# Latent attention in a two-layer encoder: rotary products, turns and key norms put into a fixed order, and two more empty products at the start

## The chip, the cores and the metric

The kernel runs on one core of a Trainium2 chip. The metric is the device time of one execution in microseconds (us). The engines are TensorE (PE, with its weight loads as PEld), VectorE (DVE), ScalarE (ACT), GpSimd (POOL) and SyncE (SP, which here only issues DMAs).

## What is computed

Two layers on a sequence of 256 positions with 1024 channels, float32. Each layer is half a SwiGLU FFN (width 2816), a mixer, and half a SwiGLU FFN, each with an RMSNorm ahead of it. The mixer of layer 0 is a convolution module; that of layer 1 is the latent attention that the change is about:

```python
def mla(h, positions, w_a, g_q, g_kv, w_uq, w_ukv, w_o):
    a = h @ w_a                                   # 512 + 256 + 64 columns
    c_q = rmsnorm(a[..., :Q_LORA], g_q)
    c_kv = rmsnorm(a[..., Q_LORA:Q_LORA + KV_LORA], g_kv)
    k_rope = a[..., Q_LORA + KV_LORA:]
    q = jnp.einsum("bsc,chd->bshd", c_q, w_uq)    # 8 heads of 128 + 64
    q_nope, q_rope = q[..., :QK_NOPE], q[..., QK_NOPE:]
    kv = jnp.einsum("bsc,chd->bshd", c_kv, w_ukv) # 8 heads of 128 + 128
    k_nope, v = kv[..., :QK_NOPE], kv[..., QK_NOPE:]
    ...
    q_rope = apply_rope(q_rope, cos[:, :, None, :], sin[:, :, None, :])
    k_rope = apply_rope(k_rope, cos, sin)
    ... # scores of both parts, block-causal softmax in chunks of 64, values
    return o.reshape(o.shape[0], seq, N_HEADS * V_HEAD) @ w_o
```

## The kernel before, in words

The 256 positions are two tiles of 128 rows, `tb` 0 and 1. Every float32 product is done as three products of split operands (`mm3`, L269, L272, L273): a weight block `raw` of 128x2048 comes by a DMA on SP's queue (1 MB), ACT writes its rounded part `hi` (L185) and DVE the rest `lo` (L186), each in two pieces of 1024 columns; the other operand is split in the same way. There are three buffers for `raw` and five for `hi` and `lo`. The weight blocks of the whole kernel are one list, in the order of their use. `weights(n, more)` takes the next n of them, and `load_ahead(k)` writes the DMAs and casts of all blocks up to k beyond those taken. For attention the list is: four blocks of `w_a`, then `wuq[2]` (rotary part of all heads), `wuq[0]` (plain part, heads 0 to 3), `wukv[0]` (keys), `wukv[1]` (values), `wuq[1]` (heads 4 to 7), and four blocks of `wo`.

The order of instructions on an engine is set by a planner: it simulates the program with costs of its own and takes, for each engine, the instruction that is ready and first in priority, which is the order in which the program is written. Functions marked `@urgent` get a higher priority. `order(a, b)` pins a behind b on the same engine; it adds no waiting on the chip. A weight cast is pinned behind the last six urgent instructions written before it on its engine (`behind`). On the chip each engine then works off its list in that order, and an instruction that waits holds up what stands behind it.

Around the change, attention goes like this. `low` makes the products with `w_a` into banks `a`: for each `tb` first the 512 query columns, then the 320 key columns. `normed` squares them on ACT (`squares`, L296), makes the factor on POOL (`power`, L304, L305, L307; `rr`, L1149), and scales on DVE (`cn`, L1151). The results are `cq[tb]` and `ck[tb]`. `key_rope` rotates the 64 shared key columns into `kd[tb]` on DVE. `split_rows` turns a normed tile: PE transposes it in pieces of 128x128 (`transposed`, L313, tile `tp`, "turns" below), ACT writes the high parts (L328) and DVE the low parts (L332), into `CQh` and `CQl` (one tile, `CQ`) for the queries and `CKh` and `CKl` for the keys. There are three banks for turns (B) and four for products (A).

Then come the rotary products `qr`, 12 for each `tb`, and `rope` on DVE (L1093, L1095, L1100), which writes `qrope`; the plain query products for four heads (`nope` into `QN`); the turns of `kd` and `qrope`; the key products (`nope` into `KN`); the values (`v`); and the scores. Before the change only the start of the rotary products was fixed by what they need; the turns, the norms and the second half of the rotary products were placed by the planner.

At its start the kernel runs `WARM` empty products (`keep_warm`, L261, 128x256, bf16, zeros) while the first weights come in.

Of the kernel before, what the change touches and what calls it, by code (L numbers as in the profile page):

```python
# [21 lines left out]
S = 256  # L22
NT = S // P
# [8 lines left out]
H = 8  # L32
NOPE = 128
ROPE = 64
VH = 128
QL = 512
KVL = 256
# [1 line left out]
EPS = 1e-6  # L39
RAW_BUFS = 3  # L40
W_BUFS = 5
WARM = 20
PIECES = 2

BEHIND = 6
# [17 lines left out]
GCOL = {}  # L63
# [19 lines left out]
def trunk(ctx: ExitStack, tc: tile.TileContext, x, xt, pos, invf, gains, gfin, wdw,  # L83
# [21 lines left out]
    def bank(tag, name):  # L105
        return ps.tile([P, 512], F32, tag=tag, name=uid(name), bufs=BANKS[tag])
# [28 lines left out]
    def order(ins, first):  # L135
        tc.add_manual_dep(ins.ins, first.name, mybir.DependencyInfo(
            mybir.DependencyClass.NoSync, mybir.DependencyReason.DATA), reason="order")
# [66 lines left out]
    def load_ahead(ahead=W_BUFS - 2):  # L204
        load_to(min(len(blocks), n_used[0] + ahead))
# [5 lines left out]
    def weights(n=1, more=True):  # L211
        out = []
        for _ in range(n):
            n_used[0] += 1
            if more:
                load_ahead()
            else:
                load_ahead(0)
            out.append(loaded[n_used[0] - 1])
        return out  # L220
# [46 lines left out]
    def mm3(o, ah, al, bh, bl, start, stop, after=()):  # L267

        mm = nc.tensor.matmul(o, ah, bl, start=start, stop=False)  # L269
        for a in after:  # L270
            order(mm, a.ins)
        nc.tensor.matmul(o, ah, bh, start=False, stop=False)  # L272
        return nc.tensor.matmul(o, al, bh, start=False, stop=stop)  # L273
# [8 lines left out]
    def tbs(tb):  # L282
        return slice(tb * P, (tb + 1) * P)
# [9 lines left out]
    def squares(ss, src, n, i, scale_in=1.0, after=()):  # L293
        nh = n // 2
        junk = tmp.tile([P, 512], F32, tag="s", name=uid("junk"))
        sq = nc.scalar.activation(junk[:, :nh], src[:, i * nh:(i + 1) * nh], AF.Square, scale=scale_in,  # L296
                                  accum_out=ss[:, i:i + 1])
        for a in after:
            order(sq, a.ins)
        return sq  # L300
# [9 lines left out]
    def transposed(src, q, n, after=(), turned=None):  # L310
        b = bank("B", "tp")
        for j in range(n):
            tp = nc.tensor.transpose(b[:, j * P:(j + 1) * P], src[:, (q + j) * P:(q + j + 1) * P], ident)  # L313
            if turned is not None:
                turned.append(tp)
            for a in after:
                order(tp, a.ins)
        return b

    @urgent  # L320
    def split_rows(src, q, n, gcol, dh, dl, tb, after=(), low_after=(), turned=None,
                   lows=None):

        b = transposed(src, q, n, after, turned)
        for j in range(n):
            k = q + j
            g = G[:, gcol + k:gcol + k + 1]
            high = nc.scalar.activation(dh[:, k, tbs(tb)], b[:, j * P:(j + 1) * P], AF.Copy, scale=g)  # L328
        for j in range(n):
            k = q + j  # L330
            g = G[:, gcol + k:gcol + k + 1]
            low = nc.vector.scalar_tensor_tensor(dl[:, k, tbs(tb)], b[:, j * P:(j + 1) * P], g,  # L332
                                                 dh[:, k, tbs(tb)].bitcast(F32), op0=ALU.mult, op1=ALU.subtract)
            if lows is not None:
                lows.append(low)
            for a in low_after:
                order(low, a.ins)
        return high
# [768 lines left out]
    def mla_in(act, X, make_next, cc, sn):  # L1107
        R = X.r
# [18 lines left out]
        def low(parts, w, tb, last):  # L1127
            u = bank("A", "a")
            for a in range(2):
                hi, lo = parts[a]  # L1130
                for j in range(4):
                    k = 4 * a + j
                    last_low[0] = mm3(u[:, :w], X.xh[:, k, tbs(tb)], X.xl[:, k, tbs(tb)], hi[:, j * w:(j + 1) * w],
                                      lo[:, j * w:(j + 1) * w], k == 0, k == KT - 1,
                                      (last,) if last is not None and k == 0 else ())
            return u

        @urgent
        def normed(u, n, tb, between=None):
            ss = small.tile([P, 2], F32, tag="ss", name=uid("ss"))  # L1140
            for i in range(2):
                sq = squares(ss, u[:, :n], n, i, R[tb])
            if between is not None:
                between()
                for high in X.highs[4:]:
                    order(high, sq.ins)
            r2 = power(ss, n, "r2")
            rr = small.tile([P, 1], F32, tag="rr", name=uid("rr"))
            nc.gpsimd.tensor_tensor(rr, r2, R[tb], op=ALU.mult)  # L1149
            cn = act.tile([P, n], F32, tag=f"cn{n}", name=uid("cn"), bufs=2)  # L1150
            scaled = nc.vector.tensor_scalar(cn, u[:, :n], rr, None, op0=ALU.mult)  # L1151
            if between is not None:
                order(scaled, X.ends[1].ins)
            return cn

        def key_rope(u, tb):
            kx = act.tile([P, 64], F32, tag="kx", name=uid("kx"), bufs=2)
            nc.vector.tensor_scalar(kx, u[:, KVL:KVL + ROPE], R[tb], None, op0=ALU.mult)
            kd = act.tile([P, 2, 64], F32, tag="kd", name=uid("kd"), bufs=2)
            for i in range(2):  # L1160
                rope(act, kd[:, i, :], kx.rearrange("p (n i f) -> p n i f", n=1, i=2), 1, cc, sn, tb)
            return kd.rearrange("p i f -> p (i f)")
# [4 lines left out]
        cq, ck, kd = [], [], []  # L1167
        last = None
        for tb in range(NT):
            for i, w in enumerate((QL, KVL + ROPE)):  # L1170
                u = low(parts[2 * i:2 * i + 2], w, tb, last)
                last = last_low[0]
                if tb == 0 and i == 1:
                    X.end(0)
                    load_ahead(1)
                if i == 0:
                    cq.append(normed(u, QL, tb))
                    if tb == 1:
                        load_ahead()
                else:  # L1180
                    if tb == 0:

                        ck.append(normed(u, KVL, tb, lambda: X.late(1)))
                    else:
                        ck.append(normed(u, KVL, tb))
                    kd.append(key_rope(u, tb))
                if tb == 1 and i == 1:
                    split_rows(cq[0], 0, 4, GCOL["q"], CQh, CQl, 0)


        QR = act.tile([P, 4, S], F32, tag="QR", name="QR")
# [1 line left out]
        QN = xp.tile([P, H, S], F32, tag="Xl", name="QN")  # L1193
        VV = act.tile([P, NT, H * VH], F32, tag="VV", name="VV")

        def nope(part, dst, nk, ch, cl, width, h0, heads):

            hi, lo = part
            for i in range(heads[0], heads[1], 2):
                b = bank("A", "nope")  # L1200
                for e in range(2):
                    for k in range(nk):
                        c = slice(k * width + (i + e) * P, k * width + (i + e + 1) * P)
                        mm3(b[:, e * S:(e + 1) * S], hi[:, c], lo[:, c], ch[:, k, :], cl[:, k, :],
                            k == 0, k == nk - 1)
                nc.scalar.copy(dst[:, h0 + i:h0 + i + 2, :], b.rearrange("p (e t) -> p e t", t=S))


        (hi, lo), = weights()
        qr = []  # L1210
        for tb in range(NT):
            u = bank("A", "qr")
            for k in range(4):
                mm3(u, CQh[:, k, tbs(tb)], CQl[:, k, tbs(tb)], hi[:, k * 512:(k + 1) * 512],
                    lo[:, k * 512:(k + 1) * 512], k == 0, k == 3)
            if tb == 0:
                lows = []
                split_rows(cq[1], 0, 4, GCOL["q"], CQh, CQl, 1, lows=lows)
                for t in range(NT):
                    split_rows(ck[t], 0, 2, GCOL["kv"], CKh, CKl, t, lows=lows)  # L1220
            q = act.tile([P, 512], F32, tag="cn512", name=uid("qrope"), bufs=2)
            rope(act, q, u.rearrange("p (n i f) -> p n i f", i=2, f=32), H, cc, sn, tb, lows)
            qr.append(q)
        part, = weights()
        nope(part, QN, 4, CQh, CQl, 512, 0, (0, 4))
        for t in range(NT):
            b = transposed(kd[t], 0, 1)
            for i in range(2):
                half = slice(64 * i, 64 * i + 64)
                nc.scalar.copy(KR[half, i, tbs(t)], b[half, :P])  # L1230
        for tb in range(NT):
            b = transposed(qr[tb], 0, 4)
            nc.scalar.copy(QR[:, :, tbs(tb)], b.rearrange("p (j t) -> p j t", t=P))
        kpart, = weights()
        nope(kpart, KN, 2, CKh, CKl, D, 0, (0, H))
# [208 lines left out]
```

## Time and profile before

| | |
|---|---|
| Runs | 929.58 us median of 3 (929.41, 929.58, 931.34) |
| Profiled execution | 931.24 us, span 929.4 us |
| PE busy | 915.6 us, 99% of the span |
| DVE, ACT, POOL busy | 589.8, 494.2, 123.6 us |
| Granted TensorE clock, mean | 0.994 |
| DMA | 194.73 MB, mean 210 GB/s |
| First rotary product | 662.31 us from the span's start |
| First key product | 682.40 us |

Times in the views are counted from the start of the span, which is 1.8 us shorter than the time of the same execution. In a timeline each row has start, duration, engine, line, operation, output<-inputs, shape and count; the bracket is the idle time of the engine before it and what ended that. Products of PE overlap, so the time that one costs is the distance from start to start. The granted clock is given as a share of full speed.

### The profile page before, as it was taken

To read this page: it belongs to the slowest core of one execution; us is meant where nothing else is said; L and a number is where in the kernel's file an instruction comes from. 1 tells how busy PE (TensorE), PEld (TensorE's weight loads), DVE (VectorE), ACT (ScalarE), POOL (GpSimd) and SP (SyncE) were. 2 spreads that over 40 slices of the span, in tenths; PEclk is the share of its full clock that TensorE was granted. 3 is DMA by queue.
4 is the path that set the end of the run, shared out by engine and by line. 5 is a ranking of instruction groups with operands and counts; after the bars stand their busy time and mean duration, and the time that the engine had idled before them with its cause. 6 is when DMAs were issued, how large, how long until landed. Compare 5 with 4: busy or idle time off the path is not lost.

```text
span 929.4 us, 12106 instructions
## 1 busy us (share of the span) xinstructions
PE 915.6 (99%) x4346; PEld 767.7 (83%) x4346; DVE 589.8 (63%) x931; ACT 494.2 (53%) x844; POOL 123.6 (13%) x255
## 2 busy tenths in 40 slices
PE   9999999999999999999999999999799999999997
PEld 7888888898978888888888888888698888888886
DVE  5895764489987666654576556545746686656633
ACT  7564544488877445443464455434846574445421
POOL 1720000079941000000010000000300010000000
PEclk9999999999999999999999999999899999999999
DMA  9887786533227667775467677654641467776711
GB/s 342 294 302 248 243 278 226 182 137 136 92 73 278 238 233 254 245 241 198 176 229 277 230 257 242 228 181 134 219 155 46 181 238 278 254 240 228 256 45 46
DMA packets 65292, 194.73 MB, mean 210 GB/s; under 512 B 11856, under 2 KB 37072, under 8 KB 45904
## 3 DMA queue, kind: packets, MB, share of 16 engines
q1 hardware_dynamic: 64656, 193.27, 59.4%
q8 instruction: 34, 0.56, 0.2%
q10 hardware_dynamic: 576, 0.69, 0.2%
q14 instruction: 26, 0.21, 0.1%
HBM read 179.78 MB, written 14.16 MB: 209 GB/s over the span
## 4 chain that ended last, share of the span: by engine, by line
PE 93%; DVE 3%; ACT 2%; POOL 1%; issue 1%; DMA 0%; POOLq 0%; ACTq 0%
PE u L273 17%; PE u L272 17%; PE u L269 17%; PE o L272 9%; PE o L269 9%; PE o L273 9%; PE gate L744 2%; DVE acc L821 2%; PE u L744 2%; PE o L985 1%; PE u L278 1%; PE tp L313 1%; PE nope L269 1%; PE nope L273 1%; PE nope L272 1%; PE sc L1253 1%
## 5 line engine op out<-in xcount | busy, mean ns | idle before, releaser
L186 DVE TENSOR_TENSOR lo<-raw,hi 128x1024 fp32r<-128x1024 f32 (+1 forms) x292 | 344.1, 1219 | 172.9 <-ACT hi L185 172.3
L185 ACT CAST hi<-raw 128x1024 fp32r<-128x1024 f32 x294 | 292.6, 1046 | 250.5 <-PE o L273 83.7
L269 PE MATMUL u<-lo,Xh 128*128 128x512 f32 x688 | 267.8, 389 | 0.0
L273 PE MATMUL u<-hi,Xl 128*128 128x512 f32 x688 | 267.8, 389 | 0.0
L272 PE MATMUL u<-hi,Xh 128*128 128x512 f32 x688 | 267.7, 389 | 0.0
L272 PEld LDWEIGHTS u<-hi,Xh 128*128 128x128 f32 x688 | 129.1, 188 | 27.0
L269 PEld LDWEIGHTS u<-lo,Xh 128*128 128x128 f32 x688 | 129.1, 188 | 26.9
L273 PEld LDWEIGHTS u<-hi,Xl 128*128 128x128 f32 x688 | 129.1, 188 | 26.8 <-DVE Xl L332 0.4
L272 PE MATMUL o<-hi,Gh 128*128 128x512 f32 (+1 forms) x356 | 137.9, 387 | 0.0
L273 PE MATMUL o<-hi,Gl 128*128 128x512 f32 (+1 forms) x356 | 137.8, 387 | 0.0
L269 PE MATMUL o<-lo,Gh 128*128 128x512 f32 (+1 forms) x356 | 137.2, 387 | 0.0
L304 POOL TENSOR_TENSOR ms<-ss 128x1 f32<-128x1 f32 x16 | 8.2, 517 | 605.4 <-ACT junk L296 605.4
L269 PEld LDWEIGHTS o<-lo,Gh 128*128 128x128 f32 x356 | 66.9, 188 | 13.6
L273 PEld LDWEIGHTS o<-hi,Gl 128*128 128x128 f32 x356 | 66.9, 188 | 13.4
L272 PEld LDWEIGHTS o<-hi,Gh 128*128 128x128 f32 x356 | 66.9, 188 | 13.4
L637 DVE TENSOR_TENSOR Gl<-gb,Gh 128x512 fp32r<-128x512 f32 (+1 forms) x48 | 31.3, 652 | 61.7 <-ACT Gh L636 61.7
L636 ACT CAST Gh<-gb 128x512 fp32r<-128x512 f32 (+1 forms) x48 | 28.0, 583 | 76.5 <-DMA gb<-gd 76.5
L821 DVE SCALAR_TENSOR_TENSOR acc<-V,dw,acc 128x128 f32<-128x128 f32 (+1 forms) x176 | 54.5, 391 | 0.0
L842 ACT ACTIVATE prod<-V,dw 128x128 f32<-128x128 f32 (+1 forms) x129 | 45.9, 415 | 1.8 <-POOL Y L843 1.0
L712 DVE TENSOR_TENSOR s<-s,u 128x512 f32<-128x512 f32 (+1 forms) x48 | 30.5, 635 | 9.8 <-PE u L273 9.8
L711 ACT ACTIVATE s<-u,R 128x512 f32<-128x512 f32 (+1 forms) x48 | 31.1, 649 | 4.6 <-PE u L273 3.9
L345 DVE STREAM_TRANSPOSE gt<-s 128x512 f32<-128x512 f32 (+1 forms) x48 | 32.0, 666 | 1.4
(213 smaller groups left out, 869.2 us busy)
## 6 DMA issues: line engine op xcount, KB each, us to landing
raw<-in_f2w SPq DMA_DIRECT2D x66, 1024.0 KB, 5.0
raw<-in_f1w SPq DMA_DIRECT2D x62, 1024.0 KB, 5.2
raw<-in_cw SPq DMA_DIRECT2D x12, 1024.0 KB, 4.7
gd<-gt SPq DMA_DIRECT2D x160, 64.0 KB, 3.4
gb<-gd SPq DMA_DIRECT2D x40, 256.0 KB, 4.6
raw<-in_wo SPq DMA_DIRECT2D x4, 1024.0 KB, 4.8
raw<-in_wuq SPq DMA_DIRECT2D x3, 1024.0 KB, 4.7
raw<-in_f1w SPq DMA_DIRECT2D x8, 256.0 KB, 5.1
```

Source lines behind the costliest of these rows:

```text
L185: casts[len(loaded), i] = (nc.scalar.copy(hi[:, c], raw[:, c]), low.tensor_sub(lo[:, c], raw[:, c], hi[:, c].bitcast(F32)))
L186: low.tensor_sub(lo[:, c], raw[:, c], hi[:, c].bitcast(F32)))
L269: mm = nc.tensor.matmul(o, ah, bl, start=start, stop=False)
L272: nc.tensor.matmul(o, ah, bh, start=False, stop=False)
L273: return nc.tensor.matmul(o, al, bh, start=False, stop=stop)
L345: nc.vector.transpose(t[:, :w], src.rearrange("p (t j q) -> p j t q", t=n, q=32))
L637: nc.vector.tensor_sub(Gl[:, f, tbs(tb)].rearrange("p t (i q) -> p t i q", q=32), bv, gh.bitcast(F32))
L711: nc.scalar.activation(s[:, :w], u[0, tb][:, :w], AF.Silu, scale=X.r[tb])
L712: nc.vector.tensor_mul(s[:, :w], s[:, :w], u[0, tb][:, w:] if both else u[1, tb])
L744: mm = nc.tensor.matmul(u[:, t], w[:, c], X.x[:, k, t], start=(k == 0), stop=(k == KT - 1))
L821: dve_last.append(nc.vector.scalar_tensor_tensor(out if j == j1 - 1 else y, v, w, y, op0=ALU.mult, op1=ALU.add))
L842: prods_last.append(nc.scalar.activation(p, v, AF.Copy, scale=w))
```

## The change

Five things are different. (1) In the loop of the low products the second key tile (`tb` 1) is only squared; the scaling, `normed`, and its `key_rope` come later. (2) The rotary products get a fixed order on PE: two k-steps of `tb` 0 (six products) behind the last low product, the four turns of `cq[1]`, the other two k-steps, and the twelve products of `tb` 1. The scaling of key norm 1 is pinned behind the low parts of `CQ` for `tb` 1. (3) The turns of both key norms are pinned behind all rotary products, and the plain query products behind those turns; the turns of `kd` and `qrope` are pinned behind the last plain query product. (4) Casts: where before three blocks were written ahead in the loop of the low products, now two are; the key block `wukv[0]` is written inside the rotary products, behind `normed` and `key_rope`, and `wukv[1]` and `wuq[1]` with the plain query products. (5) `WARM` is 22 instead of 20.

```diff
-WARM = 20
+WARM = 22
...
         @urgent
-        def normed(u, n, tb, between=None):
+        def squared(u, n, tb):
             ss = small.tile([P, 2], F32, tag="ss", name=uid("ss"))
-            for i in range(2):
-                sq = squares(ss, u[:, :n], n, i, R[tb])
-            if between is not None:
-                between()
-                for high in X.highs[4:]:
-                    order(high, sq.ins)
+            return ss, [squares(ss, u[:, :n], n, i, R[tb]) for i in range(2)]
+
+        @urgent
+        def normed(u, n, tb, ss, after=()):
             r2 = power(ss, n, "r2")
...
-            if between is not None:
-                order(scaled, X.ends[1].ins)
+            for a in after:
+                order(scaled, a.ins)
             return cn
...
         for tb in range(NT):
-            for i, w in enumerate((QL, KVL + ROPE)):
-                u = low(parts[2 * i:2 * i + 2], w, tb, last)
-                last = last_low[0]
-                if tb == 0 and i == 1:
-                    X.end(0)
-                    load_ahead(1)
-                if i == 0:
-                    cq.append(normed(u, QL, tb))
-                    if tb == 1:
-                        load_ahead()
-                else:
-                    if tb == 0:
-
-                        ck.append(normed(u, KVL, tb, lambda: X.late(1)))
-                    else:
-                        ck.append(normed(u, KVL, tb))
-                    kd.append(key_rope(u, tb))
-                if tb == 1 and i == 1:
-                    split_rows(cq[0], 0, 4, GCOL["q"], CQh, CQl, 0)
+            u = low(parts[:2], QL, tb, last)
+            cq.append(normed(u, QL, tb, squared(u, QL, tb)[0]))
+            if tb == 1:
+                load_ahead(2)
+            uk = low(parts[2:], KVL + ROPE, tb, last_low[0])
+            last = last_low[0]
+            if tb == 0:
+                X.end(0)
+                load_ahead(1)
+
+                ss, sq = squared(uk, KVL, tb)
+                X.late(1)
+                for high in X.highs[4:]:
+                    order(high, sq[1].ins)
+                ck.append(normed(uk, KVL, tb, ss, X.ends[1:]))
+                kd.append(key_rope(uk, tb))
+            else:
+                split_rows(cq[0], 0, 4, GCOL["q"], CQh, CQl, 0)
+                ss = squared(uk, KVL, tb)[0]
...
-        (hi, lo), = weights()
-        qr = []
+        (hi, lo), = weights(1, False)
+        qr, qu, lows, turned = [], [], [], []
         for tb in range(NT):
             u = bank("A", "qr")
+            qu.append(u)
             for k in range(4):
-                mm3(u, CQh[:, k, tbs(tb)], CQl[:, k, tbs(tb)], hi[:, k * 512:(k + 1) * 512],
-                    lo[:, k * 512:(k + 1) * 512], k == 0, k == 3)
-            if tb == 0:
-                lows = []
-                split_rows(cq[1], 0, 4, GCOL["q"], CQh, CQl, 1, lows=lows)
-                for t in range(NT):
-                    split_rows(ck[t], 0, 2, GCOL["kv"], CKh, CKl, t, lows=lows)
+                after = (last,) if k == 0 else turned if (tb, k) == (0, 2) else ()
+                last = mm3(u, CQh[:, k, tbs(tb)], CQl[:, k, tbs(tb)], hi[:, k * 512:(k + 1) * 512],
+                           lo[:, k * 512:(k + 1) * 512], k == 0, k == 3, after)
+                if (tb, k) == (0, 1):
+
+                    split_rows(cq[1], 0, 4, GCOL["q"], CQh, CQl, 1, (last,), (), turned, lows)
+                    ck.append(normed(uk, KVL, 1, ss, lows))
+                    kd.append(key_rope(uk, 1))
+                    load_ahead(2)
+        turned = []
+        for t in range(NT):
+            split_rows(ck[t], 0, 2, GCOL["kv"], CKh, CKl, t, (last,), lows[:4], turned, lows)
+        for tb in range(NT):
             q = act.tile([P, 512], F32, tag="cn512", name=uid("qrope"), bufs=2)
-            rope(act, q, u.rearrange("p (n i f) -> p n i f", i=2, f=32), H, cc, sn, tb, lows)
+            rope(act, q, qu[tb].rearrange("p (n i f) -> p n i f", i=2, f=32), H, cc, sn, tb, lows)
             qr.append(q)
         part, = weights()
-        nope(part, QN, 4, CQh, CQl, 512, 0, (0, 4))
+        last = nope(part, QN, 4, CQh, CQl, 512, 0, (0, 4), turned)
         for t in range(NT):
-            b = transposed(kd[t], 0, 1)
+            b = transposed(kd[t], 0, 1, (last,))
...
         for tb in range(NT):
-            b = transposed(qr[tb], 0, 4)
+            b = transposed(qr[tb], 0, 4, (last,))
```

More of the change, by code (lines that the diff above doesn't have):

```diff
@@ L1194, in mla_in, with nope @@
         VV = act.tile([P, NT, H * VH], F32, tag="VV", name="VV")
-        def nope(part, dst, nk, ch, cl, width, h0, heads):
+        def nope(part, dst, nk, ch, cl, width, h0, heads, after=()):
             hi, lo = part
@@ L1203, in nope @@
                         c = slice(k * width + (i + e) * P, k * width + (i + e + 1) * P)
-                        mm3(b[:, e * S:(e + 1) * S], hi[:, c], lo[:, c], ch[:, k, :], cl[:, k, :],
-                            k == 0, k == nk - 1)
+                        mm = mm3(b[:, e * S:(e + 1) * S], hi[:, c], lo[:, c], ch[:, k, :], cl[:, k, :],
+                                 k == 0, k == nk - 1, after if k == 0 else ())
                 nc.scalar.copy(dst[:, h0 + i:h0 + i + 2, :], b.rearrange("p (e t) -> p e t", t=S))
-        (hi, lo), = weights()
@@ L1210, in mla_in @@
-        qr = []
+            return mm
+        (hi, lo), = weights(1, False)
+        qr, qu, lows, turned = [], [], [], []
         for tb in range(NT):
             u = bank("A", "qr")
+            qu.append(u)
             for k in range(4):
-                mm3(u, CQh[:, k, tbs(tb)], CQl[:, k, tbs(tb)], hi[:, k * 512:(k + 1) * 512],
-                    lo[:, k * 512:(k + 1) * 512], k == 0, k == 3)
-            if tb == 0:
-                lows = []
-                split_rows(cq[1], 0, 4, GCOL["q"], CQh, CQl, 1, lows=lows)
-                for t in range(NT):
-                    split_rows(ck[t], 0, 2, GCOL["kv"], CKh, CKl, t, lows=lows)
+                after = (last,) if k == 0 else turned if (tb, k) == (0, 2) else ()
[6 more added lines that the diff above has]
+                    load_ahead(2)
```

## The prediction

> **What bounds the kernel now.** I read the page first (shares of the engines, the chain that ended last), then the waits of PE, then PE's timeline around the two waits that are long, then the other engines there, and the start.
>
> ```profile
> span 929.4 us, 12106 instructions
> PE 915.6 (99%) x4346; PEld 767.7 (83%) x4346; DVE 589.8 (63%) x931; ACT 494.2 (53%) x844; POOL 123.6 (13%) x255
> PE 93%; DVE 3%; ACT 2%; POOL 1%; issue 1%; DMA 0%; POOLq 0%; ACTq 0%
> ```
>
> PE is the bound over the whole span, and the chain that ended last is PE for 93%. A change gains only where PE stands still or runs slowly. The waits of PE are few:
>
> ```profile
> PE tp L313 <- DVE cn L1151: 2.4, 1, 2.4
> PE tp L313 <- DVE CKl L332: 1.9, 1, 1.9
> PE warm L261 <- DVE still L256: 1.0, 1, 1.0
> PE ms L859 <- ACT sq L853: 0.8, 1, 0.8
> PE u L278 <- ACT hi L451: 0.5, 1, 0.5
> PE qr L273 <- DVE CQ L332: 0.5, 1, 0.5
> ```
>
> Columns: total, times, longest. Three of the six, 4.8 us, are in the stretch that the diff reorders. PE's timeline there (start, duration, in brackets the idle time before it):
>
> ```profile
> 662.31 0.39 PE L269 MATMUL qr<-lo,CQ 128*128 128x512 f32 x1
> ...
> 665.06 0.82 PE L313 MATMUL tp<-ident,cn 128*128 128x128 f32 x6
> 668.32 0.44 PE L313 MATMUL tp<-ident,cn 128*128 128x128 f32 x2 [2.44 <-DVE cn L1151]
> ...
> 671.30 0.48 PE L313 MATMUL tp<-ident,kd 128*128 128x128 f32 x1 [1.88 <-DVE CKl L332]
> 672.23 0.79 PE L273 MATMUL qr<-hi,CQ 128*128 128x512 f32 x1 [0.46 <-DVE CQ L332]
> 672.83 0.63 PE L269 MATMUL qr<-lo,CQ 128*128 128x512 f32 x1
> 673.25 0.63 PE L272 MATMUL qr<-hi,CQ 128*128 128x512 f32 x1
> ...
> 677.62 0.28 PE L269 MATMUL nope<-CQ,hi 128*128 128x256 f32 x1
> ...
> 681.94 0.27 PE L313 MATMUL tp<-ident,kd 128*128 128x128 f32 x1
> 682.05 0.60 PE L313 MATMUL tp<-ident,qrope 128*128 128x128 f32 x4
> 682.40 0.36 PE L269 MATMUL nope<-CKl,hi 128*128 128x256 f32 x1
> ```
>
> The first 12 rotary products (qr) run without a gap, then six turns (tp); the next turn, of the second key norm, waits 2.44 us, and everything behind it in PE's queue waits too, though the other 12 rotary products need only the query norms. A turn of the roped key (kd) waits 1.88 us in the same way. Behind the waits the products are also slow: 672.83 to 673.25 is 0.42 us for a product of 512 columns. The windows (PE, PEld, DVE, ACT, POOL busy, then granted clock, DMA) show why:
>
> ```profile
> 669.00:676.00 7.00, 4.66 (x15) 3.48 (x15) 7.00 (x22) 2.93 (x6) 0.00 (x0) 0.52 0.76 294
> 662.31:682.40 20.09, 15.31 (x88) 12.96 (x87) 19.03 (x37) 11.83 (x24) 2.83 (x4) 0.83 0.57 210
> ```
>
> After the first long wait the granted clock is 0.52 for 7 us. From the first rotary product to the first key product (nope<-CKl) PE takes 20.09 us; DVE is busy for 19.03 of them.
>
> **The change part by part.**
>
> *The fixed order on PE.* Work between the first rotary and the first key product, at undisturbed durations: 24 rotary products at (665.06 - 662.31) / 12 = 0.229 us, 5.50; 48 nope products at (681.94 - 677.62) / 36 = 0.120, 5.76; the turns of query norm 1 (four) and of both key norms (two each), 8 at about 0.11 (five take 682.40 - 681.94 = 0.46 with the refill behind them, so 0.09 to 0.11), 0.88; and two turns of kd and four of qrope at the end, 0.57. Sum 12.71 against 20.09: 7.38 us to be had, of which 4.78 is waiting and 2.6 slow clock and refills.
>
> Is each input there in time? These rows carry it:
>
> ```profile
> 656.23 1.14 ACT L328 ACTIVATE CQ<-tp,G 128x128 fp32r<-128x128 f32 x4
> 660.00 3.89 ACT L185 CAST hi<-raw 128x1024 fp32r<-128x1024 f32 x4
> 663.79 0.36 ACT L296 ACTIVATE junk<-a,R 128x128 f32<-128x128 f32 x1
> 657.40 1.13 DVE L332 SCALAR_TENSOR_TENSOR CQ<-tp,G,CQ 128x128 fp32r<-128x128 f32 x4 [0.71 <-ACT CQ L328]
> 661.76 0.75 DVE L1151 TENSOR_SCALAR cn<-a,rr 128x512 f32<-128x512 f32 x1 [1.13 <-POOL rr L1149]
> 662.43 4.63 DVE L186 TENSOR_TENSOR lo<-raw,hi 128x1024 fp32r<-128x1024 f32 x4
> 667.77 0.48 DVE L1151 TENSOR_SCALAR cn<-a,rr 128x256 f32<-128x256 f32 x1 [0.71 <-POOL rr L1149]
> 664.94 1.03 POOL L305 TENSOR_SCALAR ms<-ms 128x1 f32<-128x1 f32 x1
> 651.50 0.19 POOL L305 TENSOR_SCALAR ms<-ms 128x1 f32<-128x1 f32 x1
> 668.37 2.35 DVE L186 TENSOR_TENSOR lo<-raw,hi 128x1024 fp32r<-128x1024 f32 x2
> 671.83 1.13 DVE L332 SCALAR_TENSOR_TENSOR CQ<-tp,G,CQ 128x128 fp32r<-128x128 f32 x4
> 673.38 0.69 DVE L1093 TENSOR_TENSOR rp<-qr,cc 128x512 f32<-128x512 f32 x1
> ```
>
> Query norm 1 is scaled at 662.5. Six rotary products end at 663.7, its four turns at 664.1, six more products at 665.5. *Casts later:* today four hi casts (two blocks) hold ACT from 660.00 to 663.89, so the squares of key norm 1, whose product ends at 662.5, start at 663.79 and end at 664.6; and four lo casts hold DVE to 667.06. With one block cast here and the other behind the key norm, ACT is free at 662.0 and DVE at about 664.8. Squares then run 662.5 to 663.3, CQ's high parts 664.3 to 665.5 (the 1.14 row), its low parts 665.5 to 666.6 (the 1.13 row; DVE began only when ACT was through). The second half of the rotary products needs the first low part at 665.9, just when it is there: 0 to 0.7 us of waiting, the upper end if the product waits for all four. They end at 668.2.
>
> *Key norms behind them.* The scaling of key norm 1 is now ordered behind CQ's low parts, so 666.6 to 667.1, if POOL has its factor. POOL took 0.19 us for a step alone and 1.03 beside the lo casts; the whole chain, squares' end to factor, was 664.6 to 667.7, 3.1 us. From 663.3 that is 666.4 even at the slow pace. The turns can go at 668.2: 1.1 us of slack, and with them the 48 nope products, which are put behind these turns although they don't need them. That is the added wait; everything PE has left queues behind it. On DVE, behind the scaling, wait the key rope (1.3 us), the moved lo casts (2.35) and later CK's low parts (1.2): all through by about 672, and the key products need them at 675.0.
>
> *Rope and banks.* The second key product pair writes the bank that the second rotary result leaves, free when DVE has read it: two ropes of about 2 us each behind 672 end at 676, and at 677 to 678 if one or two lo casts (1.22 each) get between; the pair is due at 676.5. So 0 to 1 us here; the turns of qrope can wait as long. Value projections start at 681; their block's lo casts end by 679 (2.35 behind the ropes). The DMAs stay early: both wukv loads were issued from one row at 651.46, long before their casts, and only wo, needed some 30 us later, moves with the raw buffers.
>
> ```profile
> 651.46 4.54 SPq L177 DMA_DIRECT2D raw<-in_wukv  x2
> ```
>
> I take 0.4 us for the two bounded waits together (0 to 1.7, nearer the low end, since the CQ row has a first low part 0.35 us after its start). Gain 7.38 - 0.4 = 7.0 us. Behind this stretch PE has no wait at all to the end, so nothing swallows it.
>
> *Two more empty products.* The start:
>
> ```profile
> 1.04 4.45 PE L261 MATMUL warm<-still 128*128 128x256 bf16 x20 [1.04 <-DVE still L256]
> 5.99 1.22 PE L278 MATMUL u<-hi,Xh 128*128 128x512 f32 x2 [0.50 <-ACT hi L451]
> 7.01 1.05 PE L278 MATMUL u<-lo,Xh 128*128 128x512 f32 x2
> ...
> 9.57 0.87 PE L278 MATMUL u<-lo,Xh 128*128 128x512 f32 x2
> 10.28 0.62 PE L278 MATMUL u<-hi,Xl 128*128 128x512 f32 x2
> ```
>
> Twenty end at 5.49 and the first real product waits for a cast until 5.99. Two more at 0.21 end at 5.92, inside that wait: nothing, and up to 0.4 us if in another execution the cast comes sooner. What they may bring is the clock. Ten products take 5.99 to 10.28, 4.29 us against 2.3 at full rate: 2.0 us lost, bounds of the gain 0 and 2.0. The trace shows PE busy without a break from 672.23 and the fast rate (0.23 per product) back by 676; the empty products were broken off after 4.45 us by the 0.50 us wait and did not bring it. With the wait filled the break is gone.
>
> [...]
>
> *Sum.* The profiled execution took 931.24 us for its span of 929.4; the runs are 929.41, 929.58 and 931.34, so it belongs to the slower two of four. They lie 1.7 us apart, near the 2.0 that the start can cost; I take it that the faster two had little of that loss. Against the profiled execution: 931.24 - 7.0 = 924.2 with the start as it is, and less the 1.66 by which it stands above the median, 922.6. The median itself gives the same: 929.58 - 7.0 = 922.6, and no start gain is added to it. That is the forecast; its own range is 921.0 (the whole 7.38, the lowest run, and 0.8 more by the wait on sq, or by a start without loss) to 924.3 (slow start, as in the profiled execution).
>
> **The rivals.**
>
> *A wait stays behind the key norm or the rope's banks.* Ready times above have 1.1 us of slack at the turns and none at the second key pair. For it: DVE was busy 19.03 of 20.09 us, and one lo cast slipped ahead costs 1.22. Against it: 7 us of the DVE work in the stretch (six lo casts, for blocks used from 681 on) has no need to stand before the key products (the pair at 668.37 is of that kind, for the value projection's block). With 1.5 to 3.5 us of waiting left: 924.1 to 926.1.
>
> *The gain is eaten by a wait and the slow clock.* A wait of about 2.4 us was followed by 7 us at 0.52, that is 3.4 us of lost work. If PE waits 2.4 at the key turns, 5.8 of the 7.4 are gone: 928.0, within 0.2% (1.9 us, about what a measurement of this kernel can tell from no change). The same time results if the planner, which orders what isn't pinned, puts a later wait in.
>
> *Slower: key norm 1 as the gate.* Before, PE had work that it put between the key turns; now 48 nope products stand behind them. If the scaling ends 6 us late, at 673 instead of 667.1, PE idles 4.9 to 6, and the half clock adds 3.4: 9.4 against the 7.4 gained, 931.6; from about 5.9 us of idling it is slower than 931.4. For it: POOL's 1.03 instead of 0.19, and the scaling sat behind POOL in both blocks. Against it: even at the slow pace the chain ends (666.4) before CQ's low parts let the scaling start (666.6), and with two casts less there is less to slow it.
> [...]
>
> **How the numbers follow.** Forecast 0.66; a wait stays 0.17; gain eaten 0.10; slower 0.07. Faster by over 0.2% (below 927.7) hold the first two and a little of the third: 0.84; same 0.09; slower 0.07. The range for 8 in 10 takes the forecast's and the first rival's: 920.9 to 926.1.
>
> **What would show it.** PE's timeline: no idle between the first rotary product and the first key product, that stretch 13 to 14 us instead of 20.09; turns in the order query (after six rotary products), keys (after 24), kd and qrope after the nope products; granted clock 1.00 through it; wukv's first lo casts behind key norm 1's scaling. At the start 22 empty products, the idle of 0.50 below 0.1, and products at 0.23 before 10 us. The waits list without the two tp rows. Wrong it would be if a tp row of over 1.5 us stays there, if key products wait for a rope (L1093 or L1095) or for CKl, if value products wait for a lo cast, or if a wait that did not exist before appears behind 700 us.

## The result, and the profile after

The changed kernel took 924.45 us (median of six runs, 924.39 to 925.53), the kernel before beside it 931.0 (six runs, 929.41 to 932.26): ratio 0.9934, interval 0.9921 to 0.9947. The profiled execution took 925.41 us for a span of 923.6. The page after:

```profile
span 923.6 us, 12109 instructions
PE 913.4 (99%) x4348; PEld 766.5 (83%) x4348; DVE 590.4 (64%) x931; ACT 493.5 (53%) x844; POOL 123.9 (13%) x255
PE 96%; ACT 2%; DVE 1%; issue 0%; POOL 0%; POOLq 0%; ACTq 0%; DVEq 0%
```

PE's share of the chain that ended last rose from 93% to 96%. The waits of PE after:

```profile
PE o L269 <- ACT Oh L1291: 1.7, 1, 1.7
PE warm L261 <- DVE still L256: 1.0, 1, 1.0
PE ms L859 <- ACT sq L853: 0.8, 1, 0.8
```

The two tp rows and the qr row are gone, and so is the 0.5 us at the start. A row stands there that was not in the list before: 1.7 us on `Oh`, the high part of the heads' results (values times probabilities), which the output products `o` read. PE's timeline after, from the first rotary product on:

```profile
661.64 0.39 PE L269 MATMUL qr<-lo,CQ 128*128 128x512 f32 x1
...
663.03 0.60 PE L313 MATMUL tp<-ident,cn 128*128 128x128 f32 x4
663.39 0.49 PE L269 MATMUL qr<-lo,CQ 128*128 128x512 f32 x1
...
665.33 0.42 PE L273 MATMUL qr<-hi,CQ 128*128 128x512 f32 x1
665.59 0.39 PE L269 MATMUL qr<-lo,CQ 128*128 128x512 f32 x1
...
667.65 0.60 PE L313 MATMUL tp<-ident,cn 128*128 128x128 f32 x4
668.01 0.36 PE L269 MATMUL nope<-CQ,hi 128*128 128x256 f32 x1
...
673.84 0.38 PE L313 MATMUL tp<-ident,kd 128*128 128x128 f32 x2
673.97 0.36 PE L269 MATMUL nope<-CKl,hi 128*128 128x256 f32 x1
...
681.20 0.60 PE L313 MATMUL tp<-ident,qrope 128*128 128x128 f32 x4
...
719.61 0.50 PE L269 MATMUL o<-lo,Oh 128*128 128x512 f32 x1 [1.70 <-ACT Oh L1291]
...
735.43 0.60 PE L313 MATMUL tp<-ident,h 128*128 128x128 f32 x4
```

and the window from the first rotary to the first key product:

```profile
661.64:673.97 12.33, 12.33 (x84) 11.10 (x83) 11.48 (x30) 9.23 (x19) 2.18 (x4) 1.00 0.52 171
```

PE is busy for all of 12.33 us at full granted clock, where it took 20.09 at 0.83. That is 7.76 us won. The end of attention is taken at the first turn of `h`, the input of the FFN behind it. From the first key product to there, PE took 58.83 us before (682.40 to the row below) and 61.46 after (673.97 to 735.43): 2.63 us are given back.

```profile
741.23 0.60 PE L313 MATMUL tp<-ident,h 128*128 128x128 f32 x4
```

Net of attention: 741.23 - 662.31 = 78.92 before, 735.43 - 661.64 = 73.79 after, 5.13 us. The lowest runs, measured side by side, differ by as much: 929.41 - 924.39 = 5.0.

Below, "stretch" is first rotary to first key product, "attention" first rotary product to first turn of `h`, both from one profiled execution.

### The profile page after: what moved, and what is told of

Its sections match the earlier page's. It is cut to its first block, busy times and chain, and to the rows that moved or that the text cites. A ratio compares the mean times of both kernels' runs of the same rounds, so it can differ in the third digit from the quotient of the medians.

```text
span 923.6 us, 12109 instructions
## 1 busy us (share of the span) xinstructions
PE 913.4 (99%) x4348; PEld 766.5 (83%) x4348; DVE 590.4 (64%) x931; ACT 493.5 (53%) x844; POOL 123.9 (13%) x255
## 4 chain that ended last, share of the span: by engine, by line
PE 96%; ACT 2%; DVE 1%; issue 0%; POOL 0%; POOLq 0%; ACTq 0%; DVEq 0%
PE u L269 17%; PE u L272 17%; PE u L273 17%; PE o L269 9%; PE o L272 9%; PE o L273 9%; PE u L744 3%; PE gate L744 3%; PE o L985 1%; PE u L278 1%; PE tp L313 1%; PE pairs L787 1%; PE a L273 1%; PE a L272 1%; PE a L269 1%; PE nope L269 1%
```

## The experiments

| | median | ratio to the kernel before, interval | stretch | attention |
|---|---|---|---|---|
| before | 931.0 | | 20.09 | 78.9 |
| changed | 924.45 | 0.9934, 0.9921 to 0.9947 | 12.33 | 73.8 |
| changed, again | 925.12 | 0.9942, 0.9923 to 0.9961 | 12.3 | 73.8 |
| 22 empty products alone | 930.57 | 0.9994, 0.9983 to 1.0005 | 20.0 | 78.8 |
| changed, 20 empty products | 925.55 | 0.9941, 0.9925 to 0.9957 | 12.3 | 73.8 |
| changed, casts early | 927.81 | 0.9970, 0.9957 to 0.9982 | 17.5 | 76.7 |
| casts late alone | 925.12 | 0.9938, 0.9921 to 0.9954 | 14.6 | 73.4 |
| changed, key norm late | 926.11 (one run) | | 16.1 | 75.7 |
| changed, all values first | 928.01 | 0.9971, 0.9958 to 0.9985 | 12.3 | 72.2 |
| changed, casts between | 923.37 | 0.9916, 0.9898 to 0.9933 | 12.3 | 71.8 |
| changed, key turns free | 922.44, again 922.51 | 0.9909, 0.9892 to 0.9926 | 12.6 | 71.8 |
| key turns free, casts between | 923.88 | 0.9929, 0.9909 to 0.9950 | 12.6 | 71.8 |

Each ratio is to the kernel before as it was measured beside that kernel; its medians were 931.0, 930.77, 930.65 and 930.66.

**The empty products.** Alone on the kernel before (`WARM = 22`), and taken out of the changed kernel (`WARM = 20`):

> The kernel before with 22 empty products instead of 20 and nothing else. Theory (the 0.50 us break behind the empty products holds the clock at half until about 10 us; filling it brings the full clock by about 7): the first gate product of the convolution starts near 186.5 us instead of 188.4, no idle before the first real product, and the time is 1 to 2 us below that of the kernel before, about 929.4 where the kernel before has its median of 931.0. [...]

> The changed kernel with 20 empty products instead of 22. Theory (start and attention add up, each by itself): attention as in the changed kernel, 12.3 us from the first rotary product to the first key product, and the time 1 to 2 us above the changed kernel, 925.5 to 926.5, with the idle of 0.5 us back before the first real product. Rival (the empty products do nothing): 924.4, as the changed kernel.

Alone they made no difference that can be measured: 930.57 against 930.77, twelve runs from 928.98 to 933.32 against 21 from 929.22 to 933.8. With 20 in the changed kernel the median is 925.55, 1.1 and 0.4 above the two medians with 22, with intervals that overlap. The first rows of PE with 22 alone, and then with 20 in the changed kernel:

```profile
1.04 4.22 PE L261 MATMUL warm<-still 128*128 128x256 bf16 x22 [1.04 <-DVE still L256]
5.87 0.73 PE L278 MATMUL u<-hi,Xh 128*128 128x512 f32 x2 [0.61 <-ACT hi L451]
6.60 0.73 PE L278 MATMUL u<-lo,Xh 128*128 128x512 f32 x2
```

```profile
1.04 4.45 PE L261 MATMUL warm<-still 128*128 128x256 bf16 x20 [1.04 <-DVE still L256]
5.62 1.03 PE L278 MATMUL u<-hi,Xh 128*128 128x512 f32 x2
6.49 0.63 PE L278 MATMUL u<-lo,Xh 128*128 128x512 f32 x2
```

With 22, the break is still there (0.61 us), because the products took 4.22 us, less than the 20 of before in 4.45: the clock rose in the middle of them (at 4.44 us, by the trace's record of the granted clock). With 20 in the changed kernel, the first cast came sooner, there is no break, and the fast rate (0.23 us per product) is there at 6.5 us. So in these runs neither the break nor the number of empty products went with when the clock rose, and the first cast comes at a time of its own (first real product between 5.6 and 6.6 us in these profiles). That a filled break would bring the full clock by about 7 us was the author's estimate; what decides when the clock rises was not shown.

**The casts and the order, each without the other.**

```diff
# changed, casts early
             if tb == 1:
-                load_ahead(2)
+                load_ahead()
...
-        (hi, lo), = weights(1, False)
+        (hi, lo), = weights()
...
-                    load_ahead(2)
# casts late alone, on the kernel before
                     if tb == 1:
-                        load_ahead()
+                        load_ahead(2)
...
-        (hi, lo), = weights()
+        (hi, lo), = weights(1, False)
...
                 split_rows(cq[1], 0, 4, GCOL["q"], CQh, CQl, 1, lows=lows)
+                load_ahead(2)
```

> The changed kernel with its casts written as early as before: three blocks ahead in the loop of the low products, and the values' block with the rotary products. The order on PE stays fixed. Theory (the fixed order needs the later casts, because four hi casts hold ACT and four lo casts DVE while query norm 1 and key norm 1 wait): low parts of CQ 2 us later, so PE waits 1.5 to 2.5 us in the second half of the rotary products and 0.5 to 1.5 us at the key turns, first rotary to first key product 14.5 to 16.5 us instead of 12.3, time 926.5 to 928.5. Rival (the order alone carries the gain): 12.3 to 13 us and 924.4 to 925.

> The kernel before with the casts alone moved: two blocks ahead in the loop of the low products, the key block's casts behind the split of query norm 1. PE's order is left to the planner, which puts the key turns and a turn of the roped key between the rotary products as before. Theory (the waits came from two things, casts ahead of the norms and turns ahead of products that could run): the 2.4 us wait shrinks below 1, waits at the roped key's turn and at the second half of the rotary products stay at 1 to 2 us together, first rotary to first key product 15 to 17 us, time 3 to 5 us below the kernel before. Rival A (casts alone): 13 us and the whole 6 us gain. Rival B (order alone): 20 us and no gain.

Waits of PE with the order but early casts:

```profile
PE qr L273 <- DVE CQ L332: 2.2, 1, 2.2
PE qr L269 <- ACT CQ L328: 1.1, 1, 1.1
```

and with late casts but the planner's order:

```profile
PE tp L313 <- DVE CKl L332: 0.7, 1, 0.7
PE tp L313 <- DVE cn L1151: 0.4, 1, 0.4
```

With early casts the fixed order waits for query norm 1's parts, on ACT and on DVE, 3.3 us in all; the stretch is 17.5 us, a microsecond over what was expected, and the time, 927.81, lies in the range that was expected. It is still 3.0 us below the kernel before, so the order with early casts is worth something too. The late casts alone bring the two long waits to 0.4 and 0.7 and the time to 925.12, as good as the whole change. That is the time of rival A, with a stretch (14.6) between rival A's and the theory's. So the casts alone are worth nearly all of the gain, the two parts don't add up, and the order's 2.3 us in the stretch (14.6 to 12.3) are spent again behind it, since attention as a whole is 73.4 with the casts alone and 73.8 with both.

**The wait that the change added, priced.** Fifteen more steps on POOL in the chain of key norm 1, each the factor times 1.0:

```diff
+            for _ in range(late):
+                nc.gpsimd.tensor_scalar(rr, rr, 1.0, None, op0=ALU.mult)
...
-                    ck.append(normed(uk, KVL, 1, ss, lows))
+                    ck.append(normed(uk, KVL, 1, ss, lows, 15))
```

> The changed kernel with 15 more steps on POOL (the factor times 1.0) in the chain of the second key norm, 0.27 us each, 4.0 us. It prices the wait that the change added. Theory (the scaling ended at 666.4 and the turns ran at 667.65, so 1.3 us of it are free and everything behind waits one for one): PE waits 2.4 to 2.9 us at the second key's turn, first rotary to first key product 14.7 to 15.5 us; whether the granted clock then falls to half for 3.4 us is open. Rival (PE has other work to put there): no wait over 1 us.

```profile
666.46 0.38 PE L313 MATMUL tp<-ident,cn 128*128 128x128 f32 x2
668.97 0.44 PE L313 MATMUL tp<-ident,cn 128*128 128x128 f32 x2 [2.13 <-DVE cn L1151]
...
669.94 0.42 PE L273 MATMUL nope<-CQ,lo 128*128 128x256 f32 x1
670.16 0.42 PE L269 MATMUL nope<-CQ,hi 128*128 128x256 f32 x1
```

PE waits 2.13 us at the second key's turn with 48 products behind it that need nothing from it, and then they run at 0.21 us from start to start instead of 0.12: the clock went to half for 3.41 us. The stretch is 16.1: 12.3, the wait, and 1.6 for the clock. The wait is a little under what was expected; the price of the slow clock was the open part. The planner's order behind the stretch came out otherwise here, without the wait on `Oh`, so that attention is only 1.9 us longer and the single run 1.0 to 1.7 us above the changed kernel's medians.

**The new wait on Oh.** In the changed kernel ACT and PE have, around it:

```profile
715.40 3.88 ACT L185 CAST hi<-raw 128x1024 fp32r<-128x1024 f32 x4
716.27 0.38 PE L1290 MATMUL pv<-ptT,VV 128*128 128x128 f32 x2
719.18 0.37 ACT L1291 CAST Oh<-pv 128x256 fp32r<-128x256 f32 x1
```

Four hi casts, for weights of the FFN behind attention, stand ahead of the fourth head's high part, whose values (`pv`) PE had ready at 716.65. First all steps of that kind were marked urgent:

```diff
-            nc.scalar.copy(Oh[:, hd, :], b[:, :S])
-            nc.vector.tensor_sub(Ol[:, hd, :], b[:, :S], Oh[:, hd, :].bitcast(F32))
+            urgent(nc.scalar.copy)(Oh[:, hd, :], b[:, :S])
+            urgent(nc.vector.tensor_sub)(Ol[:, hd, :], b[:, :S], Oh[:, hd, :].bitcast(F32))
```

> The changed kernel, with the two steps that empty the bank of the values (high part on ACT, low part on DVE) marked urgent, so that weight casts written later stand behind them. Theory (the new wait of 1.7 us on Oh comes from four hi casts that the planner put ahead of one of these steps, and eats that much of the gain): wait gone, first rotary product to the first turn of h behind attention 72.1 us instead of 73.8, time 1.5 to 1.8 us below the changed kernel of the same call. Rival (the casts are then late themselves, or another step of the scores waits): 0 to 0.5 us below it, with a new wait in the list.

The wait went and attention took 72.2 us, but casts that were then late (two lo casts on DVE, 734.80 to 737.15) stood ahead of the low part of the FFN's input, `Xl`. The row below is new, half clock for 3.41 us followed it, and the time rose to 928.01. The rival had the new wait, but neither it nor the theory had the time, 2.9 us above the changed kernel measured beside it.

```profile
PE u L273 <- DVE Xl L332: 2.9, 1, 2.9
```

Then the casts were spread, a pair behind each of three heads; PE's order stays row for row that of the changed kernel:

```diff
-        return o.finish(None, make_next, act)
+        nxt = o.finish(None, make_next, act)
+        for n, hd in ((13, 3), (14, 4), (15, 5)):
+            for i in range(PIECES):
+                order(casts[base + n, i][0], emptied[hd].ins)
+        return nxt
```

> The changed kernel with the three pairs of hi casts behind attention pinned one pair behind each of the fourth, fifth and sixth head's high part (Oh), instead of two pairs ahead of the fourth. PE's order is the same, row for row. Theory (the 1.7 us wait on Oh is those two pairs of casts, 3.9 us on ACT, and nothing else holds PE there): no wait on Oh, first rotary product to first turn of h 72.1 us instead of 73.8, no new wait in the FFN behind it, time 1.5 to 1.9 us below the changed kernel, 922.6 to 923.5. Rival (the wait moves to another head or, as with all values first, into the FFN): a wait of 1 to 3 us on Oh or on Xl, time as the changed kernel.

```profile
PE warm L261 <- DVE still L256: 1.0, 1, 1.0
PE u L278 <- ACT hi L451: 0.8, 1, 0.8
PE ms L859 <- ACT sq L853: 0.8, 1, 0.8
```

```profile
732.04 0.60 PE L313 MATMUL tp<-ident,h 128*128 128x128 f32 x4
```

```profile
715.30 0.37 ACT L1292 CAST Oh<-pv 128x256 fp32r<-128x256 f32 x1 [1.17 <-PE pv L1291]
715.57 0.49 ACT L1285 COPY ptT<-tp 128x384 f32<-128x384 f32 x1
715.95 2.01 ACT L185 CAST hi<-raw 128x1024 fp32r<-128x1024 f32 x2
```

ACT now waits for the fourth head's values and casts behind them. There is no wait in attention, which takes 732.04 - 660.26 = 71.78 us, 2.0 less than in the changed kernel: the wait of 1.7 and 0.3 around it (the first product behind the wait took 0.50 us instead of 0.39). The medians differ by 1.1 and 1.75 from the two of the changed kernel (five runs here, 922.04 to 923.9), the lowest runs by 2.0 to 2.35. That the casts ahead of that one step made the wait is shown; the exact size in the median is not, at this spread. It also shows what the order is worth on top of the late casts once nothing eats it: attention 71.8 instead of 73.4, lowest run 922.04 instead of 924.12.

**The pins on the key turns.**

```diff
-            split_rows(ck[t], 0, 2, GCOL["kv"], CKh, CKl, t, (last,), lows[:4], turned, lows)
+            split_rows(ck[t], 0, 2, GCOL["kv"], CKh, CKl, t, lows=lows)
```

> The changed kernel without the pins that put the key turns behind all rotary products and the plain query products behind the key turns; the order of the rotary products, the casts and the urgent marks stay. The planner then puts the first key's turns among those of query norm 1, and plain products between the rotary ones. Theory (with the casts later the inputs are in time, so this pin is worth little): no PE wait over 0.5 us there, first rotary to first key product 12.2 to 13.2 us, time within 0.7 us of the changed kernel. Rival (the pin keeps PE from waiting for the second key norm): a wait of 1 to 2.5 us at a key turn and 1 to 3 us more time.

> The changed kernel again, beside the others of this call. Theory (the two more empty products are worth nothing that can be measured, as the run with them alone says): 924.4 to 925.6, overlapping the 925.55 of the changed kernel with 20 empty products. Rival (they are worth the 1.1 us between 924.45 and 925.55): 924.4 with little spread.

> The kernel without the two pins on the key turns once more, beside the one with the casts between. Theory (its lead over the changed kernel was only the missing wait on Oh, since its stretch up to the first key product is 0.3 us longer): 922.4 to 923, level with the changed kernel with the casts between. Rival (the free key turns are worth something of their own): 1 us or more below it.

> Both: the key turns without their pins and the casts between. Theory (there is no wait on Oh without the pins, so nothing is left for the casts): the same as without the pins alone, 922.4 to 923. Rival (the two add): 1 us or more below both.

Without the pins there is no wait in the stretch, which is 0.3 us longer (12.6), and none on `Oh`: the planner's order behind it came out otherwise. Neither the theory nor the rival of the first run had that. 922.44 and again 922.51 are the lowest medians here, 1.9 to 2.7 below the changed kernel; the intervals of the first pair (0.9892 to 0.9926 against 0.9923 to 0.9961) barely touch. The kernel with the casts between is level with it in attention (71.8 both) and in the lowest run (922.04, against 922.04 and 922.12), and 0.9 above it in the median, with intervals that overlap. Both changes together took nothing further off; its profiled execution, 928.3 us, had 10.24 us of half clock ahead of attention, and its median is not better than either alone; its lowest run, 922.26, and its attention, 71.8, are level with the others. So the pins on the key turns cost about 2 us in the time. There is no wait in the stretch with them or without, and taking away only the wait on `Oh` brings the same, so the cost came through what the planner did with ACT's casts 45 us later. Without the pins the planner put the four hi casts ahead of the fifth head (ACT, 717.64 to 721.52), as in the kernel before, and PE did not wait.

## Why the prediction held, and where its steps were off

The forecast was 922.6 in 920.9 to 926.1; measured were 924.45 and 925.12. Both lie above the forecast's own band (921.0 to 924.3) and in that of its first rival (924.1 to 926.1), whose mechanism, a wait that stays in the stretch, did not come. So the range held in part by luck: the rival's width covered a wait of another kind.

- *Stretch: right, a little low.* 12.71 us of work and 0.4 of waiting were expected, 12.33 came. One set of four `qrope` turns (0.44), counted in the 12.71, ran behind the first key product instead. The second half of the rotary products waited 0.03 us for `CQ` (665.33 to 665.59, 0.26 instead of 0.23), the bank of the rope nothing.
- *Key norm as the gate: right in place and slack.* The rows of DVE and POOL after:

```profile
664.84 1.13 DVE L332 SCALAR_TENSOR_TENSOR CQ<-tp,G,CQ 128x128 fp32r<-128x128 f32 x4 [0.85 <-ACT CQ L328]
665.88 0.48 DVE L1149 TENSOR_SCALAR cn<-a,rr 128x256 f32<-128x256 f32 x1
```

```profile
662.79 1.25 POOL L304 TENSOR_TENSOR ms<-ss 128x1 f32<-128x1 f32 x1 [1.85 <-ACT junk L296]
665.03 0.19 POOL L1147 TENSOR_TENSOR rr<-r,R 128x1 f32<-128x1 f32 x1
```

  The factor was there at 665.2, the scaling ran right behind `CQ`'s low parts and ended at 666.36, 1.3 us ahead of the turns at 667.65 (1.1 expected). One POOL step took 1.25 us while two lo casts ran (661.64 to 663.99), the others 0.19 to 0.55, and as the forecast had it, this cost nothing here. The slower rival's mechanism was right too: with the key norm late there was a wait of 2.13 us and then half clock for 3.41 us, which cost 1.6 us (the rival had 3.4 for a longer wait).
- *"Behind this stretch PE has no wait at all to the end, so nothing swallows it": the step that failed.* It was read from the trace of before, for an order of ACT that the planner then made anew. Before, four hi casts stood ahead of the fifth head, whose values were ready only at 727.63, as the casts ended:

```profile
723.81 3.88 ACT L185 CAST hi<-raw 128x1024 fp32r<-128x1024 f32 x4
727.25 0.38 PE L1284 MATMUL pv<-ptT,VV 128*128 128x128 f32 x2
727.67 0.37 ACT L1285 CAST Oh<-pv 128x256 fp32r<-128x256 f32 x1
```

  After, they stood ahead of the fourth, and PE waited 1.7 us. With the 0.3 around it this wait took 2.0 of the 2.63 us given back, as the run with the casts between shows (59.45 us from the first key product to the first turn of `h`, instead of 61.46). The other 0.6 is mostly work that only changed its place, the set of `qrope` turns. The prediction had named the sign itself: a wait that did not exist before, behind 700 us. It was the second rival's last sentence, a later wait put in by the planner, at about a third of the size given there (2.0 of 5.8).
- *Which part carries it: not asked finely enough.* The sum put the gain on the fixed order and took the later casts as what makes it possible. The runs say that the casts alone bring the whole net gain, and the order with early casts 3.0 us.
- *Start: the term was wrong, and did not enter the sum.* The profiled execution of before did lose 2.0 us there, and 22 products can be run with a break or without. But it was the exception: by the traces' records the clock first rose between 3.73 and 6.39 us in the other twelve executions, whether with 20 products or 22, and at 10.09 in this one. And the 1.7 us between the runs of before can't be put down to it, since with 22 products alone the spread is the same. Half clock in other places adds to it, below.
- *Sum: near by luck.* 7.0 us were forecast between medians, 6.55 came, and 5.5 when both were measured again; between lowest runs it is 5.0, the net of attention. The medians stand 1.6 us above the lowest run before and 0.06 after (1.1 when measured again). The granted clock of each run goes with this: where it is on record, runs of the kernel before took 929.2 to 931.3 us at a mean clock of 0.996 and 933.3 to 933.8 at 0.989, runs of the changed kernel 924.0 to 924.5 at 0.998 and 927.3 to 927.7 at 0.992. So what the 6.55 has above 5.0 goes, by these runs, with half clock that varies from run to run; that the change has a part in it was not shown. A slip in the sum: the lower end of the forecast's own band adds up to 921.2 (929.41 - 7.38 - 0.8), not 921.0.

## What to carry to other kernels

Where a planner orders each engine, a gain in one place is to be followed to the end of the stage in the order that comes out, because casts and copies on the other engines are dealt anew; the waits of the trace before say nothing about them. Ahead of pinning PE's order, look at what keeps the inputs late: here the casts of two blocks, written later, were worth as much as the whole change. A pin that puts work behind a step which it doesn't need buys an exact order at the price of that step's lateness, and here of a wait elsewhere.

## What the runs showed of the chip

The changed kernel's profiled execution had half clock where that of before had none, in the convolution, behind the sums of one column:

```profile
248.66 2.35 PE L859 MATMUL ms<-ones,sq 128*128 128x1 f32 x16
250.87 3.59 PE L744 MATMUL u<-Xp,raw 128*128 128x128 f32 x16
```

```profile
252.00:254.00 2.00, 2.00 (x11) 2.00 (x11) 1.27 (x5) 0.99 (x3) 2.00 (x6) 0.50 0.00 0
```

The same 16 products took 2.03 us before:

```profile
250.65 2.35 PE L859 MATMUL ms<-ones,sq 128*128 128x1 f32 x16
252.86 2.03 PE L744 MATMUL u<-Xp,raw 128*128 128x128 f32 x16
```

Nothing of the change lies there. Half clock stood at this place in six of the 13 profiled executions, all six of kernels with the changed attention (ten of the 13 are); in the other seven the granted clock was 1.00 from 248 to 264 us. It lasted 3.41, 6.83 or 10.24 us: 3.41 and 10.24 in two executions of the changed kernel, 6.83 and 3.41 in two of the kernel with the key turns free. So its length at one place differs between executions of one kernel. No long wait of PE stands ahead of it: in the changed kernel PE was busy for 1.93 of the 2.00 us from 248 to 250, mostly in these sums.

Half clock also came behind waits of PE: 6.83 us of it behind the wait of 2.44 us in attention of the kernel before, 3.41 behind the 2.13 with the key norm late and the 2.86 on `Xl` with all values first. Behind the 1.70 on `Oh` there was none, the granted clock was 1.00 from 719.6 to 735.4.

What brings the half clock in the convolution in six executions and not in the other seven was not shown, nor whether the change has a part in it; a run that changes the sums was not made. What brings the full clock back was not shown either.

With no half clock between the start and the last 2.7 us, the profiled executions took 922.04 (casts between) and 924.67 (casts late alone, with the first product 1.0 us late).
